# Two transformer layers on one core: three kinds of loads are ordered behind a transpose, and layer 2's first raw weights get a buffer of their own

## The chip, the cores and the metric

The kernel runs on one core of a Trainium2 chip. The metric is the device time of one execution in microseconds (us); lower is better. The engines are TensorE (PE in the profile, its weight loads PEld), VectorE (DVE), ScalarE (ACT), GpSimd (POOL) and SyncE (SP). All DMA transfers of this kernel are issued by SP, from one queue and in order.

## The reference, cut to what matters

```python
D_MODEL = 1024; SEQ = 1024; DEPTH = 2; HEAD_DIM = 64; N_HEADS = 16; BLOCK = 128
DSWA_GROUPS = ((128, 1), (512, 4), (2048, 16))

def reference(x, positions, ...):
    for i in range(DEPTH):
        h = rms_norm(x, norm_g[i])
        if i == 0:
            o, gate = fox_mixer(h, ...)      # layer 1
        else:
            o, gate = dsw_mixer(h, ...)      # layer 2
        x = x + (o * silu(gate)) @ w_out

def fox_mixer(h, w_in, b_f, q_g, k_g):       # q, k, v, gate and forget logits from h @ w_in
    c = cumsum(log_sigmoid(f_logit), axis=1)
    # causal, per head:  p = softmax(q k^T / 8 + c_q - c_k);  o = p v

def dsw_mixer(h, cos, sin, w_in, q_g, k_g):  # q, k, v for each of three dilated windows
    # per window g: rotary q and k, banded softmax with its log-sum-exp, o_g = p v
    # o = sum over g of softmax_g(lse_g) * o_g
```

Everything is float32. The kernel reaches that precision with a high and a low part of each operand.

## The kernel before, in words

The sequence is eight tiles of 128 rows. The projections use the input transposed (`xh`, `xl`: high and low part). A "unit" is one slab of 384 weight columns (q, k and v of a pair of heads) projected for the eight tiles: `project` does 24 matmuls per tile, and a unit has 192 of them.

Layer 1 (the "fox" layer, up to about 660 us with its output projection) has eight such units, one per head pair `hp`. Besides the projection, TensorE works on the attention of head pairs whose projections are done: scores `s` (L450), whose bias row `bc` (L624, the cumulated forget logits of one head, broadcast to 128 partitions) VectorE adds while it takes the maximum (L658); ScalarE's exponential; the split of the exponentials into f16 high and low (`ph`, ScalarE L495 and GpSimd L498); a DMA transpose of `ph` into `ptt` (L499, in `p_transpose`); and the product with the values (`o`, L506 to L508). Query tile t needs t + 1 blocks of keys, so tile 7 has the largest transposes: one of 128x16x128 for each head of the pair, first e = 0, then e = 1. Queries and keys reach TensorE by another DMA transpose, `hl` into `qk_t` (L430, made for two tiles at a time).

Layer 2 (the dilated windows) has 24 units: eight of window 0, and then for each head pair one of window 2 and one of window 1. A transpose `ptt` is made there too (L913). The sum over windows uses `og_d` and `cmb`. The unit that ends window 0 reads the input again in another order (`reload_x`: tiles `x2`). The last unit, for the output projection, loads rows of the mixed result (`turn_y`: tiles `yt`, 128x512, L711) and TensorE transposes them (L346).

Each unit's weights come in four loads of 384 KB, `load(0)` to `load(3)`, into tiles `raw` (two buffers), in the unit before the one that uses them. VectorE takes a maximum of each (`bound`, `vm`, L258), and each half of a `raw` is split into a high and a low part (`w`: ScalarE L289, then GpSimd or VectorE L291).

What sets the order: on TensorE the order is that of the program, written by hand with a clock of ticks (`Flow`): a tile's projection is four ticks, and `flow.at(slot, fn)` puts a piece of work at a tick. The order on the other engines, SP's queue among them, is set by a scheduler with its own estimates. Each tag of a pool has a fixed number of buffers: the tag `ga` holds `bc` (layer 1, 7 buffers), and in layer 2 `x2` and `yt` (4 buffers). A DMA waits for the work that fills its source and for the last readers of the buffer that it overwrites; what stands behind it in SP's queue waits with it.

Of the kernel before, what the change touches and what calls it, by code (L numbers as in the profile page):

```python
# [2 lines left out]

# [1 line left out]

# [17 lines left out]
P = 128  # L23
# [3 lines left out]
NT = S // P  # L27
NH = 16
HD = 64
NHP = NH // 2  # L30
# [52 lines left out]
def trunk(ctx, tc, ins, out, cfg):  # L83
    nc = tc.nc
# [20 lines left out]
    flow = Flow()  # L105

    layer = {}

    def next_layer(bufs):
        if layer:  # L110
# [5 lines left out]
    def lay(shape, dtype, name, tag):  # L116
        return layer["pool"].tile(shape, dtype, name=name, tag=tag, bufs=layer["bufs"][tag])
# [9 lines left out]
    c_d = dram.tile([NH, S], F32, name="c_d")  # L127
# [110 lines left out]
    class Weights:  # L238
# [7 lines left out]
                self.vm2 = sm.tile([P, KT // 2], F32R, name="vm2", tag="vm2")  # L246

        def load(self, i, tag=None):
            if tag is None:
                self.raw[i] = w_p.tile([P, 2, 384], F32, name="raw", tag="raw", bufs=2)  # L250
            else:
                self.raw[i] = lay([P, 2, 384], F32, name="raw", tag=tag)
            nc.sync.dma_start(self.raw[i][:, :, : self.n], self.src[:, 2 * i : 2 * i + 2, :])

        def bound(self, i):
            if self.vcols is None:
# [230 lines left out]
    def p_transpose(ne, nk, exps, splits):  # L487

        ph = lay([P, ne, 2, nk], F16, name="ph", tag="ph")
        pt = lay([P, ne * 2 * nk // P, P], F16, name="ptt", tag="ptt")  # L490
        for p, acc in exps:
            nc.scalar.activation(p, p, AF.Exp, bias=acc, scale=-1.0)  # L492
        for e, cols, p, pool_l in splits:
            if cfg["ph"]:
                nc.scalar.copy(ph[:, e, 0, cols], p)  # L495
            else:
                nc.vector.tensor_copy(ph[:, e, 0, cols], p)
            (nc.gpsimd if pool_l else nc.vector).tensor_sub(ph[:, e, 1, cols], p, ph[:, e, 0, cols])  # L498
        nc.sync.dma_start_transpose(pt, ph.rearrange("p e a k -> p (e a k)"))  # L499
        return pt.rearrange("p (e a k) s -> p e a k s", a=2, e=ne)  # L500

    def pv(o, e, blocks, vt):
# [116 lines left out]
    bcs = {}  # L619

    def load_bc(hp, h, es=(0, 1)):
        for e in es:
            bcs[hp, e, h] = lay([P, 512], F32, name="bc", tag="ga")
            nc.sync.dma_start(bcs[hp, e, h], c_d[2 * hp + e, h * 512 : (h + 1) * 512].partition_broadcast(P))  # L624

    def fox_tile(hp, t, kts, vt, sl):
        LP = cfg["lpf"]
        nk = (t + 1) * P
        st = {}
        pieces = [(a, min(a + 512, nk)) for a in range(0, nk, 512)]  # L630
        both = len(pieces) == 1
        accs = {}
        ptl = {}
        ps = {0: [], 1: []}

        def score(e, c):
            a, b = pieces[c]
            if e == 0 and c == 0:
                gs = st["gs"] = lay([P, P], F32, name="gsf", tag="gsl")
                nc.sync.dma_start(gs, gs_d[t * P : (t + 1) * P, hp * P : (hp + 1) * P])  # L640
            if c == 0:
                accs[e] = BIG
                st["acc"] = sm.tile([P, 2], F32, name="acc", tag="acc", bufs=8)
            if t < 2:
                if e == 0:
                    st["p"] = lay([P, 2, nk], F32, name="p", tag="p")
                p = st["p"][:, e]
            else:
                p = lay([P, b - a], F32, name="p", tag="p")
            ps[e].append(p)  # L650
            s = ps_s.tile([P, 512], F32, name="s", tag="s")
            runs = [(kts[j // 2], j % 2, n) for j, n in key_runs(range(a // P, b // P))]
            scores(s, kts[t // 2], t % 2, e, runs, b < nk)
            if b == nk:

                nc.tensor.matmul(s[:, t * P - a : b - a], ident_b, tri_b, start=False, stop=True, skip_group_check=True)
            acc = st["acc"][:, c : c + 1]
            nc.vector.tensor_tensor_reduce(p, s[:, : b - a], bcs[hp, e, a // 512][:, : b - a], -1.0, accs[e], ALU.add, ALU.min, acc)  # L658
            accs[e] = acc
            pl = (cfg["pl"] & 1, cfg["pl"] >> 1 & 1)  # L660
            if c < len(pieces) - 1 or both and e == 0:
                return
            if both:
                exps = [(ps[i][0], accs[i]) for i in range(2)]
                if t < 2:
                    splits = [(slice(0, 2), slice(0, nk), st["p"], pl[1])]
                else:
                    splits = [(i, slice(0, nk), ps[i][0], pl[i]) for i in range(2)]
                pt = p_transpose(2, nk, exps, splits)
                for i in range(2):  # L670
                    ptl[i] = [(pt[:, i, 0, j], pt[:, i, 1, j], j) for j in range(t + 1)]
            else:
                exps = [(p, accs[e]) for p in ps[e]]
                splits = [(0, slice(*pieces[i]), ps[e][i], pl[i]) for i in range(2)]
                pt = p_transpose(1, nk, exps, splits)
                ptl[e] = [(pt[:, 0, 0, j], pt[:, 0, 1, j], j) for j in range(t + 1)]

        def values(e):
            if e == 0:
                st["o"] = ps_o.tile([P, 2, HD + 1], F32, name="o", tag="o")  # L680
            pv(st["o"], e, ptl[e], vt)
            if e == 1:
                finish()

        def finish():
            o = st["o"]
            rec = sm.tile([P, 2], F32, name="rec", tag="rec")
            nc.vector.reciprocal(rec, o[:, :, HD])
            y = sb.tile([P, P], F32, name="y", tag="y")
            for e in range(2):  # L690
                nc.vector.scalar_tensor_tensor(y[:, e * HD : (e + 1) * HD], o[:, e, :HD], rec[:, e : e + 1], st["gs"][:, e * HD : (e + 1) * HD], ALU.mult, ALU.mult)
            if hp == NHP - 1:
                turn_last(y, t, flow.now + 3)
            else:
                nc.sync.dma_start(y_d[t * P : (t + 1) * P, hp * P : (hp + 1) * P], y)


        ts, tv = cfg["fox"][both]
        for e in range(2):
            for c in range(len(pieces)):  # L700
                urgent(lambda e=e, c=c: score(e, c), "ps", sl + ts[e * len(pieces) + c])
            urgent(lambda e=e: values(e), "pv", sl + LP + tv[e])
# [29 lines left out]
    for hp in range(NHP):  # L732
        w2 = (fox_weights(hp + 1) if hp + 1 < NHP else part(w_fo, 0)).ahead()
        s0 = flow.now
        if hp == 0:
            load_bc(0, 0)
        for h, e, slot in cfg["bc"]:
            if hp + 1 - h < NHP:
                flow.at(s0 + slot, lambda n=hp + 1 - h, h=h, e=e: load_bc(n, h, (e,)))
        kts = []  # L740
        vt = v_tile(w.vs)
        vsr = sm.tile([P, NT], F32, name="vsr", tag="vsr")
        nc.scalar.activation(vsr, rx[:, 0], AF.Copy, scale=w.vs)
        for t in range(NT):
            ps = project(w, tile_cols(0, t))
            if t % 2 == 0:
                hd = heads_begin()
            heads_tile(ps, 0, t, hd, vt, vsr[:, t : t + 1], rx[:, 2, t - 1 : t + 1])
            if t % 2:
                with tc.high_priority(cfg["ph_"]):  # L750

                    turn = heads_pair(0, t - 1, hd)
                    flow.at(flow.now + (6 if hp < NHP - 1 else 4), lambda turn=turn, kts=kts: kts.append(turn()))
                for i in range(2):

                    tt = t - 1 + i
                    fox_tile(hp, tt, kts, vt, s0 + (cfg["due"][tt] if hp < NHP - 1 else 4 * tt + 18))
            if hp == NHP - 1:

                a = max(flow.now + 1, s0 + cfg["due"][t] - 4 * NT + cfg["lpf"] + 9)  # L760
                turn_y(t, 0, [(flow.now + 1, flow.now + 8), (a, a + 7)])
        w = w2
# [229 lines left out]
    for ci, (hp, g) in enumerate(order):  # L992
        w2 = (dsw_weights(ci + 1) if ci + 1 < len(order) else part(w_do, 0)).ahead()
        vt = v_tile(w.vs)
# [3 lines left out]
        for t in range(NT):  # L998
            if ci == NHP - 1:
                reload_x(t)  # L1000
            ps = project(w, tile_cols(g, t))
# [20 lines left out]
            else:  # L1022
                cmb = {}
# [31 lines left out]
    layer["cm"].__exit__(None, None, None)  # L1055


CFG = dict(pin=1, bc=((1, 0, 26), (1, 1, 28), (0, 0, 38), (0, 1, 46)), wl=(0x50, 0x50), ps=0, pv=100, ph_=100, ph=1, wbufs=12, pl=3, um=3, lpf=8, lsd=((16, 16), (16, 14), (14, 11)), ty2=((0, 4), (1, 5)), hb=1, ub=2, qb=1, nb=3, fox=(((0, 0, 2, 2), (2, 4)), ((0, 0), (4, 4))), due=(29, 33, 39, 45, 35, 41, 49, 57), l1=dict(ga=7, ptt=3, ph=2, p=4, qk_t=6, vt=3, gsl=3), l2=dict(ga=4, cmb=3, ptt=3, ph=2, p=2, qk_t=3, og=3, vt=3, gsl=3, par=1), wload=(0, 4, 13, 20), wbound=(9, 14, 22, 27), wscale=28, wsplit=(10, 11, 15, 16, 29, 29, 30, 30))


def host_layout(inputs):
# [49 lines left out]
```

## Time and profile before

| | |
|---|---|
| median of 3 runs | 1816.11 us (1810.0 to 1819.2) |
| profiled execution | 1818.5 us, span 1816.7 us |
| TensorE | busy 1737.0 us, 96% of the span |
| VectorE, ScalarE, GpSimd | 60%, 56%, 54% |
| DMA, from SP's queue | 652996 packets, 288.36 MB, 71.4% of the 16 engines' span |
| layer 1's attention units | 193 to 468 us |
| layer 2's units of windows 2 and 1 | 1082 to 1717 us, the output projection from there to the end |

How to read the rows that follow: a row of the timeline has the start in us, the duration, the engine and line, the operation with its output and input tiles, and in brackets the idle time of that engine just before and what ended it. On SP ("SPq") the duration is that of issuing a DMA, not of its transfer. A granted clock of 1.00 is TensorE's full clock.

### The profile page before, as it was taken

How to read it: one execution, taken by the hardware profiler on the slowest of the kernel's cores; microseconds unless marked ns; L12 is line 12 of the kernel's file. 1: busy time of each engine (PE TensorE's matmuls, PEld its weight loads, DVE VectorE, ACT ScalarE, POOL GpSimd, SP SyncE). 2: the span in 40 equal slices, each digit the busy share in tenths (PEclk: the TensorE clock that was granted, in tenths of full speed). 3: DMA queues.
4: the chain of work that ended last, by engine and by line, in shares of the span. 5: the costliest groups of instructions: out<-in, count | busy, mean ns of one | idle time of the engine just before them, and what ended most of it. 6: DMA issues, size and time to landing. Idle time of an engine off the chain costs nothing.

```text
span 1816.7 us, 38150 instructions
## 1 busy us (share of the span) xinstructions
PE 1737.0 (96%) x13276; PEld 1641.7 (90%) x13276; DVE 1093.3 (60%) x3674; ACT 1011.0 (56%) x2696; POOL 973.5 (54%) x1175
## 2 busy tenths in 40 slices
PE   7999999999988989999999999999999999999999
PEld 6999888888876779999999989999999999999877
DVE  8546666666664453365556585666675666667631
ACT  6536666666665465455555665555555555555620
POOL 4215565556545431255656566667576666757530
PEclk9999999999999999999999999999999999999999
DMA  8447999999999763456767687667677776667852
GB/s 285 127 130 140 193 190 185 176 177 183 187 190 207 213 188 114 127 113 134 142 133 144 146 191 143 157 140 152 138 163 144 162 151 143 149 140 179 189 154 85
DMA packets 653189, 290.79 MB, mean 160 GB/s; under 512 B 512306, under 2 KB 616754, under 8 KB 652996
## 3 DMA queue, kind: packets, MB, share of 16 engines
q1 hardware_dynamic: 652996, 288.36, 71.4%
q8 instruction: 104, 1.70, 0.4%
q14 instruction: 89, 0.73, 0.1%
HBM read 126.46 MB, written 37.03 MB: 90 GB/s over the span
## 4 chain that ended last, share of the span: by engine, by line
PE 45%; DMA 12%; DVE 6%; ACT 4%; issue 3%; POOL 3%; SPq 1%; DVEq 0%; POOLq 0%; ACTq 0%
PE pj L313 33%; PE pj L336 7%; DMA raw<-in_w_dsw 5%; PE s L450 2%; DMA qk_t<-hl 2%; DMA ptt<-ph 2%; DMA og_d<-og 1%; POOL hl L425 1%; POOL w L291 1%; DMA cmb<-og_d 1%; DVE w L291 1%; DVE hl L426 1%; DVE u L422 1%; PE ob L506 1%; DVE p L906 1%
## 5 line engine op out<-in xcount | busy, mean ns | idle before, releaser
L313 PE MATMUL pj<-w,xh 128*128 128x384 f32 (+2 forms) x4864 | 1259.6, 341 | 30.2 <-ACT w L289 7.3
L313 PEld LDWEIGHTS pj<-w,xh 128*128 128x128 f32 x4864 | 873.1, 191 | 38.9 <-DVE ge L481 7.8
L313 PE MATMUL pj<-w,xl 128*128 128x384 f32 (+2 forms) x2432 | 817.6, 336 | 0.2 <-DVE xl L530 0.2
L313 PEld LDWEIGHTS pj<-w,xl 128*128 128x128 f32 x2432 | 464.7, 191 | 0.9 <-DVE xl L530 0.9
L291 POOL TENSOR_TENSOR w<-raw,w 128x384 fp32r<-128x384 f32 (+2 forms) x258 | 261.7, 1035 | 233.3 <-ACT w L289 228.8
L498 POOL TENSOR_TENSOR ph<-p,ph 128x512 f16<-128x512 f32 (+3 forms) x176 | 172.9, 999 | 161.9 <-ACT ph L495 160.7
L289 ACT CAST w<-raw 128x384 fp32r<-128x384 f32 (+2 forms) x352 | 162.6, 501 | 114.8 <-PE pj L336 37.4
L425 POOL TENSOR_TENSOR hl<-u,hl 128x512 f16<-128x512 f32 x128 | 151.2, 1181 | 125.0 <-ACT hl L424 124.9
L912 POOL TENSOR_TENSOR ph<-p,ph 128x768 f16<-128x768 f32 (+2 forms) x96 | 155.3, 1618 | 102.9 <-ACT ph L911 102.9
L383 ACT ACTIVATE sq<-pj 128x256 f32<-128x256 f32 x256 | 97.2, 380 | 168.9 <-DVE u L378 167.2
L450 PE MATMUL s<-qk_t 128*128 128x128 f16 (+1 forms) x1504 | 162.0, 248 | 19.2 <-DVE acc L658 10.4
L336 PE MATMUL pj<-xh,w 128*128 128x512 f32 x512 | 170.4, 404 | 2.2 <-ACT p L907 1.1
L258 DVE TENSOR_REDUCE vm<-raw 128x1 f32<-128x256 f32 x128 | 53.6, 419 | 156.2 <-DMA raw<-in_w_dsw 118.6
L506 PEld LDWEIGHTS <-ptt 128*128 128x128 f16 x1136 | 102.9, 98 | 48.8 <-issue 27.5
L389 DVE SCALAR_TENSOR_TENSOR vt<-pj,vsr,vt 128x128 f16<-128x128 f32 x256 | 89.6, 350 | 93.2 <-ACT vt L388 92.8
L450 PEld LDWEIGHTS <-qk_t 128*128 128x128 f16 x1504 | 110.2, 98 | 36.1 <-issue 22.0
L424 ACT CAST hl<-u 128x512 f16<-128x512 f32 x128 | 79.2, 619 | 104.9 <-DVE u L422 88.6
L495 ACT CAST ph<-p 128x512 f16<-128x512 f32 (+3 forms) x176 | 88.9, 537 | 72.7 <-DMA ptt<-ph 72.3
L492 ACT ACTIVATE p<-p,acc 128x512 f32<-128x512 f32 (+2 forms) x192 | 109.0, 609 | 30.6 <-DVE acc L658 27.4
L336 PEld LDWEIGHTS pj<-xh,w 128*128 128x128 f32 x512 | 97.6, 191 | 24.5 <-DVE xr L779 1.5
L378 DVE TENSOR_TENSOR u<-pj,gr 128x256 f32<-128x256 f32 x256 | 106.4, 416 | 18.4 <-PE pj L313 18.3
L907 ACT ACTIVATE p<-p,og 128x128 f32<-128x128 f32 (+1 forms) x256 | 98.1, 441 | 33.6 <-DVE og L906 33.4
(171 smaller groups left out, 2609.4 us busy)
## 6 DMA issues: line engine op xcount, KB each, us to landing
raw<-in_w_dsw SPq DMA_DIRECT2D x96, 384.0 KB, 3.7
raw<-in_w_fox SPq DMA_DIRECT2D x32, 384.0 KB, 3.7
og_d<-og SPq DMA_DIRECT2D x64, 132.0 KB, 3.2
cmb<-og_d SPq DMA_DIRECT2D x64, 132.0 KB, 3.3
bc<-c_d SPq DMA_DIRECT2D x32, 256.0 KB, 3.9
gs_d<-ge SPq DMA_DIRECT2D x32, 192.0 KB, 3.2
xt<-in_xt SPq DMA_DIRECT2D x16, 256.0 KB, 6.1
xrow<-in_x SPq DMA_DIRECT2D x8, 512.0 KB, 6.3
```

Of the source, the lines that this page charges most:

```text
L289: nc.scalar.copy(w[:, 0, :n], raw[:, k % 2, :n])
L291: eng.tensor_sub(w[:, 1, :n], raw[:, k % 2, :n], w[:, 0, :n].bitcast(F32))
L313: nc.tensor.matmul(ps[:, :n], a[:, k, cols], w.slabs[k][:, j, :n], start=(k == 0 and i == 0), stop=(k == KT - 1 and i == 2))
L336: nc.tensor.matmul(ps[m], w.slabs[k][:, j, m * P : (m + 1) * P], a[:, k, 512 * b : 512 * (b + 1)], start=(k == 0 and x == 0), stop=(k == K ...
L378: nc.vector.tensor_mul(u[:, t % 2].rearrange("p (a b) d -> p a b d", a=2), ps[:, : 4 * HD].rearrange("p (a b d) -> p a b d", a=2, b=2), gr ...
L425: nc.gpsimd.tensor_sub(hl[:, :, :4, 1], u, hl[:, :, :4, 0])
L450: nc.tensor.matmul(s[:, c0 : c0 + cnt * P].rearrange("p (c s) -> p c s", c=cnt), qk[:, i, blk], kk[:, j : j + cnt, e], start=(h == 0), sto ...
L492: nc.scalar.activation(p, p, AF.Exp, bias=acc, scale=-1.0)
L498: (nc.gpsimd if pool_l else nc.vector).tensor_sub(ph[:, e, 1, cols], p, ph[:, e, 0, cols])
L506: nc.tensor.matmul(o[:, e, :], hi, vt[:, j, e, HD:], start=(b == 0), stop=False, skip_group_check=True)
L907: nc.scalar.activation(p[:, e], p[:, e], AF.Exp, bias=acc[:, e : e + 1], scale=-1.0)
L912: nc.gpsimd.tensor_sub(ph[:, 1], st["p"], ph[:, 0])
```

## The change

`tc.issue_after(x)` orders what is issued inside it behind the instruction x on the same queue; it adds no wait. The change keeps the transpose `ptt` of tile 7, e = 1 of the latest head pair in `last["late"]`, and puts behind it, on SP: the first weight load of each unit, the `bc` loads of the first half of the sequence (h = 0), and the `qk_t` transpose of tiles 6 and 7. `last["late"]` keeps its value in layer 2, where it has long been issued. In layer 2 `load(0)` goes to a tag of its own, `raw0`, with one buffer, so a unit has three `raw` buffers in place of two, and `ga` shrinks from four buffers to two.

```diff
+    def queued():
+        return tc.issue_after(last["late"]) if "late" in last else nullcontext()
...
         def load(self, i, tag=None):
+            if i == 0 and tag is None and "raw0" in layer["bufs"]:
+                tag = "raw0"
             if tag is None:
                 self.raw[i] = w_p.tile([P, 2, 384], F32, name="raw", tag="raw", bufs=2)
             else:
                 self.raw[i] = lay([P, 2, 384], F32, name="raw", tag=tag)
-            nc.sync.dma_start(self.raw[i][:, :, : self.n], self.src[:, 2 * i : 2 * i + 2, :])
+            with queued() if i == 0 else nullcontext():
+                nc.sync.dma_start(self.raw[i][:, :, : self.n], self.src[:, 2 * i : 2 * i + 2, :])
...
-        nc.sync.dma_start_transpose(pt, ph.rearrange("p e a k -> p (e a k)"))
+        last["ptt"] = nc.sync.dma_start_transpose(pt, ph.rearrange("p e a k -> p (e a k)")).ins
...
             bcs[hp, e, h] = lay([P, 512], F32, name="bc", tag="ga")
-            nc.sync.dma_start(bcs[hp, e, h], c_d[...].partition_broadcast(P))
+            with queued() if h == 0 else nullcontext():
+                nc.sync.dma_start(bcs[hp, e, h], c_d[...].partition_broadcast(P))
...
                 pt = p_transpose(1, nk, exps, splits)
+                if t == NT - 1 and e == 1:
+                    last["late"] = last["ptt"]
...
-                    flow.at(flow.now + (6 if hp < NHP - 1 else 4), lambda turn=turn, kts=kts: kts.append(turn()))
+                def turned_keys(turn=turn, kts=kts, t=t):
+                    with queued() if t == NT - 1 else nullcontext():
+                        kts.append(turn())
+                flow.at(flow.now + (6 if hp < NHP - 1 else 4), turned_keys)
...
-... l2=dict(ga=4, cmb=3, ptt=3, ... par=1), ...
+... l2=dict(ga=2, cmb=3, ptt=3, ... par=1, raw0=1), ...
```

TensorE's order of instructions is the same before and after. The scheduler sets the others anew. Line numbers of the changed kernel are up to 17 higher (L430 is L439, L499 is L508, L624 is L634, L253 is L262).

Place one: SP's queue at the end of a layer 1 unit (near 245 us in the trace). `ptt_3286` and `ptt_3347` are tile 7's two transposes, e = 0 and e = 1; `raw_3500` is a unit's first weight load. Before:

```order
L640 DMA gsf_3421<-gs_d_88 128x128
L624 DMA bc_3666<-c_d_87 128x512
L624 DMA bc_3907<-c_d_87 128x512
L624 DMA bc_4239<-c_d_87 128x512
L430 DMA_TRANSPOSE qk_t_3455<-hl_3224 128x12x128
L695 DMA y_d_83<-y_3411 128x128
L499 DMA_TRANSPOSE ptt_3286<-ph_3285 128x16x128
L253 DMA raw_3500<-in_w_fox 128x768
L499 DMA_TRANSPOSE ptt_3347<-ph_3346 128x16x128
L499 DMA_TRANSPOSE ptt_3437<-ph_3436 128x4x128
```

and after:

```order
L650 DMA gsf_3421<-gs_d_88 128x128
L439 DMA_TRANSPOSE qk_t_3455<-hl_3224 128x12x128
L707 DMA y_d_83<-y_3411 128x128
L508 DMA_TRANSPOSE ptt_3286<-ph_3285 128x16x128
L650 DMA gsf_3502<-gs_d_88 128x128
L508 DMA_TRANSPOSE ptt_3347<-ph_3346 128x16x128
L508 DMA_TRANSPOSE ptt_3437<-ph_3436 128x4x128
L262 DMA raw_3500<-in_w_fox 128x768
L262 DMA raw_3592<-in_w_fox 128x768
L634 DMA bc_3666<-c_d_87 128x512
L634 DMA bc_3907<-c_d_87 128x512
```

Three `bc` loads and the first weight load have moved behind tile 7's transposes; `qk_t_3455` and the `y` store stay ahead of them.

Place two: GpSimd in a unit of window 1 of layer 2 (near 1396 to 1405 us). `ra`, `rb` and the line that writes `u` are the rotary step; `w_20120` to `w_20173` are low parts of the next unit's weights, of which `raw_19960` is the first load. Before:

```order
L940 TENSOR_TENSOR cmb_19747<-cmb_19747 128x4x65
L410 TENSOR_TENSOR ra_19928<-u_19838,cs_114 128x128
L411 TENSOR_TENSOR rb_19929<-u_19838,sn_115 128x8x8
L412 TENSOR_TENSOR rb_19929<-u_19838,sn_115 128x8x8
L936 TENSOR_TENSOR wt_20131<-mm_20129,cmb_19897 128x12
L413 TENSOR_TENSOR u_19838<-ra_19928,rb_19929 128x8x16
L912 TENSOR_TENSOR ph_19916<-p_19896,ph_19916 128x768
```

and after:

```order
L957 TENSOR_TENSOR cmb_19747<-cmb_19747 128x4x65
L300 TENSOR_TENSOR w_20120<-raw_19960,w_20120 128x384
L419 TENSOR_TENSOR ra_19928<-u_19838,cs_114 128x128
L420 TENSOR_TENSOR rb_19929<-u_19838,sn_115 128x8x8
L421 TENSOR_TENSOR rb_19929<-u_19838,sn_115 128x8x8
L300 TENSOR_TENSOR w_20136<-raw_19960,w_20136 128x384
L953 TENSOR_TENSOR wt_20131<-mm_20129,cmb_19897 128x12
L929 TENSOR_TENSOR ph_19916<-p_19896,ph_19916 128x768
L300 TENSOR_TENSOR w_20173<-raw_19991,w_20173 128x384
L422 TENSOR_TENSOR u_19838<-ra_19928,rb_19929 128x8x16
```

Three weight splits and the split of the exponentials now stand ahead of the last step of the rotary.

Place three: SP's queue in the last unit (near 1685 us). `yt_24248` and `yt_24259` are rows of tile 1, `yt_24405` and `yt_24407` those of tile 2. Before, tile 1's two loads stand far ahead, and here is:

```order
L430 DMA_TRANSPOSE qk_t_24088<-hl_24083 128x12x128
L913 DMA_TRANSPOSE ptt_24198<-ph_24197 128x8x128
L711 DMA yt_24405<-y_d_83 128x512
L711 DMA yt_24407<-y_d_83 128x384
L430 DMA_TRANSPOSE qk_t_24226<-hl_24221 128x12x128
L1018 DMA og_d_89<-og_24040 128x264
```

and after:

```order
L439 DMA_TRANSPOSE qk_t_24088<-hl_24083 128x12x128
L930 DMA_TRANSPOSE ptt_24198<-ph_24197 128x8x128
L723 DMA yt_24248<-y_d_83 128x512
L723 DMA yt_24259<-y_d_83 128x384
L439 DMA_TRANSPOSE qk_t_24226<-hl_24221 128x12x128
L1035 DMA og_d_89<-og_24040 128x264
L723 DMA yt_24405<-y_d_83 128x512
L723 DMA yt_24407<-y_d_83 128x384
```

Tile 1's loads stand where tile 2's stood, since only two `yt` are held at a time.

More of the change, by code (lines that the diff above doesn't have):

```diff
@@ L1 @@
 import heapq
-from contextlib import ExitStack
+from contextlib import ExitStack, nullcontext
 import numpy as np
@@ L107, in trunk @@
     layer = {}
+    last = {}
+    def queued():
+        return tc.issue_after(last["late"]) if "late" in last else nullcontext()
     def next_layer(bufs):
@@ L623, in load_bc @@
             bcs[hp, e, h] = lay([P, 512], F32, name="bc", tag="ga")
-            nc.sync.dma_start(bcs[hp, e, h], c_d[2 * hp + e, h * 512 : (h + 1) * 512].partition_broadcast(P))
+            with queued() if h == 0 else nullcontext():
+                nc.sync.dma_start(bcs[hp, e, h], c_d[2 * hp + e, h * 512 : (h + 1) * 512].partition_broadcast(P))
     def fox_tile(hp, t, kts, vt, sl):
@@ L1055, in trunk @@
     layer["cm"].__exit__(None, None, None)
-CFG = dict(pin=1, bc=((1, 0, 26), (1, 1, 28), (0, 0, 38), (0, 1, 46)), wl=(0x50, 0x50), ps=0, pv=100, ph_=100, ph=1, wbufs=12, pl=3, um=3, lpf=8, lsd=((16, 16), (16, 14), (14, 11)), ty2=((0, 4), (1, 5)), hb=1, ub=2, qb=1, nb=3, fox=(((0, 0, 2, 2), (2, 4)), ((0, 0), (4, 4))), due=(29, 33, 39, 45, 35, 41, 49, 57), l1=dict(ga=7, ptt=3, ph=2, p=4, qk_t=6, vt=3, gsl=3), l2=dict(ga=4, cmb=3, ptt=3, ph=2, p=2, qk_t=3, og=3, vt=3, gsl=3, par=1), wload=(0, 4, 13, 20), wbound=(9, 14, 22, 27), wscale=28, wsplit=(10, 11, 15, 16, 29, 29, 30, 30))
+CFG = dict(pin=1, bc=((1, 0, 26), (1, 1, 28), (0, 0, 38), (0, 1, 46)), wl=(0x50, 0x50), ps=0, pv=100, ph_=100, ph=1, wbufs=12, pl=3, um=3, lpf=8, lsd=((16, 16), (16, 14), (14, 11)), ty2=((0, 4), (1, 5)), hb=1, ub=2, qb=1, nb=3, fox=(((0, 0, 2, 2), (2, 4)), ((0, 0), (4, 4))), due=(29, 33, 39, 45, 35, 41, 49, 57), l1=dict(ga=7, ptt=3, ph=2, p=4, qk_t=6, vt=3, gsl=3), l2=dict(ga=2, cmb=3, ptt=3, ph=2, p=2, qk_t=3, og=3, vt=3, gsl=3, par=1, raw0=1), wload=(0, 4, 13, 20), wbound=(9, 14, 22, 27), wscale=28, wsplit=(10, 11, 15, 16, 29, 29, 30, 30))
 def host_layout(inputs):
```

## The prediction

> **What bounds the kernel now.** I read the page's busy times first, then the chain, then what TensorE waits for.
>
> ```profile
> span 1816.7 us, 38150 instructions
> PE 1737.0 (96%) x13276; PEld 1641.7 (90%) x13276; DVE 1093.3 (60%) x3674; ACT 1011.0 (56%) x2696; POOL 973.5 (54%) x1175
> ...
> PE pj L313 33%; PE pj L336 7%; DMA raw<-in_w_dsw 5%; PE s L450 2%; DMA qk_t<-hl 2%; DMA ptt<-ph 2%; DMA og_d<-og 1%; POOL hl L425 1%; POOL w L291 1%; DMA cmb<-og_d 1%; DVE w L291 1%; DVE hl L426 1%; DVE u L422 1%; PE ob L506 1%; DVE p L906 1%
> ```
>
> TensorE bounds it. Nothing in the change takes a matmul away, so all that can be gained is its idle time, 1816.7 - 1737.0 = 79.7 us, and the matmuls that run slow because the clock has dropped. The chain names loads and transposes that the change moves, but only with 2 to 5% each. The waits of TensorE by cause (us in all, times, longest):
>
> ```profile
> PE o L506 <- DMA ptt<-ph: 16.8, 11, 3.6
> PE s L450 <- DVE acc L658: 10.4, 10, 2.0
> ...
> PE pj L313 <- DVE u L422: 6.0, 7, 1.6
> ```
>
> The largest is the one that the first part of the change is near: the product with the values waiting for a transpose. Where in layer 1 the idle time lies is told by a table by unit (start and end, length, then busy time of PE, and at the end of the row the granted clock, the busy share of the DMA engines and GB/s):
>
> ```profile
> 143.76:192.93 49.17, 48.73 (x458) 45.64 (x458) 33.28 (x122) 33.00 (x83) 28.68 (x30) 1.00 0.90 179
> 192.93:247.35 54.42, 50.62 (x506) 47.09 (x506) 35.42 (x127) 35.22 (x91) 32.48 (x33) 1.00 0.98 186
> 247.35:301.40 54.05, 50.76 (x507) 47.22 (x507) 34.63 (x124) 34.46 (x87) 31.69 (x33) 1.00 0.94 184
> 301.40:357.25 55.85, 51.99 (x506) 48.61 (x506) 35.89 (x130) 35.38 (x91) 32.78 (x33) 0.97 0.90 181
> ...
> 411.45:467.76 56.31, 52.04 (x506) 48.55 (x506) 36.68 (x130) 36.35 (x93) 33.51 (x34) 0.97 0.98 181
> ```
>
> Each of the last four has 3.3 to 4.3 us of idle time. Two of them have a lower clock as well, and their PE time is 1.3 us longer for the same 506 matmuls. The timeline shows why (TensorE rows, idle time before them in brackets):
>
> ```profile
> 252.63 0.20 PE L506 MATMUL o<-vt,ptt 128*128 128x65 f16 x1 [1.36 <-DMA ptt<-ph]
> ...
> 308.26 0.20 PE L506 MATMUL o<-vt,ptt 128*128 128x65 f16 x1 [2.92 <-DMA ptt<-ph]
> ...
> 311.99 0.80 PE L313 MATMUL pj<-w,xh 128*128 128x384 f32 x2
> 312.63 0.34 PE L313 MATMUL pj<-w,xl 128*128 128x384 f32 x1
> 312.80 0.52 PE L313 MATMUL pj<-w,xh 128*128 128x384 f32 x2
> ...
> 417.82 0.20 PE L506 MATMUL o<-vt,ptt 128*128 128x65 f16 x1 [2.46 <-DMA ptt<-ph]
> ```
>
> After the wait of 1.36 us nothing happens to the clock. After 2.92 us a pair of matmuls takes 0.80 us until 312.8, and 0.52 from there: the last slow ones of a stretch of about 3.4 us, in which matmuls run at half the rate, about 1.5 us lost. The wait of 2.46 us is followed by the same stretch. So I price a wait of over some 2 us at 1.5 us more.
>
> The Trainium skill ("TensorE: Matmul & The Clock Gate", the table of what matters for kernels) asks for no idle gaps over about 3 us, and Part 1 gives an idle window of about 3.4 us ahead of half rate. Here 2.46 us was enough, so the trace differs. By the page neither of these waits would cost more than itself, and the sum below would be a gain of 2.6 - 1.5 = 1.1 us without the clock in layer 1, and 1.1 + 1.5 = 2.6 us if the page is kept in the tail as well.
>
> **The change part by part.** *Layer 1, the queue.* SP's rows ahead of the wait at 252.63, and VectorE's wait behind the same load:
>
> ```profile
> 241.97 1.33 SPq L624 DMA_DIRECT2D bc<-c_d  x3
> 245.56 1.43 SPq L430 DMA_TRANSPOSE qk_t<-hl  x1
> 247.08 1.11 SPq L695 DMA_DIRECT2D y_d<-y  x1
> 248.28 1.84 SPq L499 DMA_TRANSPOSE ptt<-ph  x1
> 250.22 1.02 SPq L253 DMA_DIRECT2D raw<-in_w_fox  x1
> 251.34 4.40 SPq L499 DMA_TRANSPOSE ptt<-ph  x2
> ...
> 254.54 0.42 DVE L258 TENSOR_REDUCE vm<-raw 128x1 f32<-128x256 f32 x1 [3.19 <-DMA raw<-in_w_fox]
> ```
>
> Two things move: three `bc` loads of 256 KB from ahead of the first transpose of tile 7, and the weight load from between the two. The second is plain: the weight load's 1.02 us of issue go from ahead of the second transpose, and that transpose's own issue (two rows in 4.40 us, of which 1.20 is the small one) should fall from 3.1 to about 1.8 us, as the first has. That brings e = 1 some 2 us earlier. But TensorE hardly waits for it: 252.63 is e = 0. For e = 0 the three stay that stand right ahead (`qk_t`, `y`, itself), 1.43 + 1.11 + 1.84 = 4.38 us; only the transfers of `bc`, still under way when `qk_t` is issued, go. In the unit from 301.40 the last two took 0.53 and 1.32 us, so up to 1.1 us of this is backlog of the DMA engines; transposes keep these 0.9 to 0.98 busy in any case, so I take half, 0.6 us, at six unit ends: 3.6 us. I add one clock stretch (the wait of 2.46 us comes under 2 us): 1.5 us. VectorE's 3.19 us wait for the weights goes from this place, and `acc` with it; of the 10.4 us that TensorE waits for `acc` I take 0.5. Layer 1: -5.6 us. Bounds: no gain at all, if the engines' backlog stays; and five waits (10 us, two of 2.92 and 2.46 among them) gone with both stretches and 2 us of `acc`, -15.
>
> The moved loads have cover. A unit's first weights are split some 10 ticks later and used a unit later (50 us); `bc` for the first half is used from the next unit's middle; `qk_t` of tiles 6 and 7 is used by tile 6 and 7's scores, the next unit's work. Should the cover of the second weight pair fail (its buffer waits for the splits of the first, now later), the transposes behind it on SP are held up by about 1 us: within the bounds.
>
> *Layer 2, first weights a unit ahead.* Rows of a unit of window 1:
>
> ```profile
> 1395.86 2.35 POOL L291 TENSOR_TENSOR w<-raw,w 128x384 fp32r<-128x384 f32 x2
> 1398.55 0.89 SPq L253 DMA_DIRECT2D raw<-in_w_dsw  x2
> 1400.03 0.48 POOL L413 TENSOR_TENSOR u<-ra,rb 128x128 f32<-128x128 f32 x1
> 1401.06 1.66 POOL L912 TENSOR_TENSOR ph<-p,ph 128x768 f16<-128x768 f32 x1 [0.56 <-ACT ph L911]
> 1403.97 0.42 DVE L258 TENSOR_REDUCE vm<-raw 128x1 f32<-128x256 f32 x1 [0.58 <-DMA raw<-in_w_dsw]
> 1405.11 0.69 DVE L422 TENSOR_TENSOR u<-u,pj 128x512 f32<-128x512 f32 x1
> 1405.94 0.60 PE L313 MATMUL pj<-w,xh 128*128 128x384 f32 x2 [1.58 <-DVE u L422]
> ...
> 1160.00:1670.00 510.00, 501.36 (x3728) 489.39 (x3726) 345.65 (x1284) 283.05 (x863) 346.15 (x476) 1.00 0.69 151
> ```
>
> Two loads are issued together, VectorE waits for both, and the rotary product behind it is late for TensorE. With the first load a unit ahead, the second still comes in at the same place, so `vm` of it still waits to about 1403. And the early weights let the scheduler put their splits ahead of the rotary on GpSimd. From its free time at 1398.9 (0.75 us of `cmb` after the row at 1395.86): one split 0.97, rotary 1.13, split and `wt` 1.20, `ph` 1.66, split 0.97, then the last step 0.48: it ends at 1405.3 in place of 1400.5, about where VectorE starts the product now. So the wait changes its cause more than its size. In thirteen units from 1160 to 1670 all idle time is 510.00 - 501.36 = 8.6 us. I take -1.5; bounds -7 and +4.
>
> *Layer 2, two buffers for `x2`.* In the unit from 1036 to 1082 us each `x2` load must wait for the splits of two loads before. That chain (a load of about 3.5 us, a copy and a subtraction of 0.6 and 0.7) is about as long as a tile's 5.2 us of projection. SP's other work queues behind those waits. +1, bounds 0 and +3.
>
> *Layer 2, two buffers for `yt`.* The loads of tile 1 move from 1649 to 1653 to the place after the transpose at 1684.84:
>
> ```profile
> 1653.32 1.00 SPq L711 DMA_DIRECT2D yt<-y_d  x1
> ...
> 1684.84 1.23 SPq L913 DMA_TRANSPOSE ptt<-ph  x1
> 1686.17 1.01 SPq L711 DMA_DIRECT2D yt<-y_d  x2
> ...
> 1685.92 0.63 PE L346 MATMUL pt<-ident,yt 128*128 128x128 f32 x4
> ...
> 1712.59 1.09 PE L346 MATMUL pt<-ident,yt 128*128 128x128 f32 x4 [2.61 <-issue]
> ...
> DMA to landing us min/median/max: 2.3/3.5/4.8
> ```
>
> TensorE turns tile 1 at 1685.92. With the load issued at 1686.2 and 3.4 us to land, it waits to about 1689.5: 3.6 us, long enough for a clock stretch, 1.5 more. Part comes back, since work that waits later (2.61 us at 1712.59) gets time: I take 1.6. Net +3.5; bounds +1 and +6.
>
> Sum: -5.6 - 1.5 + 1 + 3.5 = -2.6 us. The profiled execution took 1818.5 us (1.8 around its span), so 1815.9 for such a one; it stands 2.4 above the median of 1816.1, so 1813.5.
>
> **The rivals.** (1) *Nothing in layer 1.* For it: the DMA engines are 0.90 to 0.98 busy there, and order does not make less work; also `qk_t` and `y` stay ahead of e = 0. Against it: the waits are latency of one transfer, and VectorE's wait of 3.19 us does go. Then 3.0 in layer 2 alone: -1.5 + 1 + 3.5, 1819 us.
>
> (2) *All of the waits for tile 7 go.* For it: the issue of 1.84 and 3.1 us against 1.2 for the small transpose shows a backlog, and both long waits bring clock stretches with them. -15 in layer 1, -3 in layer 2's units, +1, +3.5: -13.5, so 1818.5 - 13.5 - 2.4 = 1802.6.
>
> (3) *Slower: the rotary behind the splits.* Place: GpSimd's last rotary step in the units of window 1. It decides once this step ends 0.5 us later than 1405.3, for then TensorE's 1.58 us become over 2 and the clock drops: 0.5 + 1.5 = 2 us in each of eight units, 16 us. 1813.5 + 16 = 1829.5. For it: the sum of durations above leaves no slack. Against it: the scheduler may have kept the slack in other units, and the wait for `vm` ends nearly 1 us earlier (its load is now issued first, at 1398.55).
>
> **How the numbers follow.** About 0.5%, 9 us, is what a measurement of this kernel can tell from no change (the three runs lie 9 us apart). My forecast has 0.45, rival 1 0.20, rival 2 0.22, rival 3 0.13. Faster than 1807: rival 2 and 0.05 from the forecast's lower edge, 0.27. Slower than 1825: rival 3, 0.13. The rest, 0.60, is within. The range takes in rival 1 and most of rival 2's side, and leaves rival 3 and the extreme of 2 out: 1804 to 1822.
>
> **What would show it.** Right: in the units from 193 to 468 us TensorE waits for `ptt` under 2 us each and the two clocks of 0.97 become nearer to 1; the second transpose of tile 7 is issued in under 2 us; VectorE no longer waits 3 us for `in_w_fox` there; near 1686 us a new wait of about 3.6 us of TensorE's transposes for `yt`; in window 1's units the wait for the rotary stays between 1 and 2 us. It is wrong if the waits for `ptt` keep their size (rival 1), vanish (2), or if the sum of waits for the rotary grows past 12 us (3).

## The result, and the profile after

The changed kernel is slower: 1826.82 us in the median of 15 runs (1820.19 to 1832.84) against 1815.52 of 15 runs before; the ratio is 1.0061, with an interval from 1.0050 to 1.0072. I had forecast 1813.5, within 1804 to 1822. The profiled execution has a span of 1828.2 us, 11.5 more than before. The page's busy times, and the waits of TensorE (us in all, times, longest):

```profile
span 1828.2 us, 38050 instructions
PE 1741.3 (95%) x13276; PEld 1647.4 (90%) x13276; DVE 1091.4 (60%) x3674; ACT 1011.6 (55%) x2696; POOL 977.6 (53%) x1175
```

```profile
PE o L515 <- DMA ptt<-ph: 17.1, 8, 3.8
PE s L459 <- DMA qk_t<-hl: 13.8, 9, 2.6
PE s L459 <- DVE acc L668: 10.0, 9, 1.7
PE pt L355 <- DMA yt<-y_d: 6.7, 3, 2.8
...
PE pj L322 <- DVE u L431: 1.3, 3, 0.7
```

Two of these rows before the change:

```profile
PE s L450 <- DMA qk_t<-hl: 3.5, 5, 1.2
...
PE pt L346 <- DMA yt<-y_d: 2.1, 1, 2.1
```

The wait for the transposed exponentials, at which the first part of the change is aimed, has not shrunk (16.8 before). The wait for the rotary product has (6.0 to 1.3). In its place stand waits for `qk_t`, 13.8 us against 3.5 (7.0 of them in the units from 1126 to 1675 us, 5.6 in the two units before), and for `yt`, 6.7 against 2.1 (the new one of 2.8 in the last unit; the other two are in layer 1's output projection). TensorE itself is busy 4.3 us longer with the same matmuls: more of them run at the lower clock (mean granted clock 0.985 against 0.990).

Four stretches of the same work, first before, then after (start and end, length, PE busy, and at the end clock, DMA share, GB/s). They are five units of layer 1, the `x2` unit with its successor, the units up to the last, and the last:

```profile
192.93:467.76 274.83, 256.07 (x2526) 238.59 (x2526) 177.21 (x631) 175.99 (x444) 162.39 (x162) 0.99 0.95 183
```

```profile
1036.27:1122.42 86.15, 82.20 (x653) 80.00 (x651) 61.20 (x189) 55.49 (x148) 52.48 (x61) 0.98 0.77 167
1122.42:1668.93 546.51, 537.84 (x3994) 525.04 (x3992) 365.03 (x1368) 303.30 (x925) 365.05 (x505) 1.00 0.69 151
1668.93:1717.00 48.07, 44.53 (x319) 42.58 (x317) 30.95 (x103) 28.80 (x82) 24.84 (x35) 0.96 0.84 182
```

```profile
192.81:467.24 274.43, 257.02 (x2526) 240.26 (x2526) 179.43 (x631) 175.25 (x442) 161.76 (x161) 0.98 0.93 184
```

```profile
1034.19:1126.08 91.89, 83.98 (x653) 81.09 (x651) 62.18 (x189) 56.25 (x150) 51.25 (x61) 0.96 0.80 164
1126.08:1675.22 549.14, 538.85 (x3994) 526.52 (x3992) 358.88 (x1365) 302.81 (x924) 366.24 (x504) 1.00 0.68 149
1675.22:1728.33 53.11, 46.91 (x319) 44.80 (x317) 30.33 (x101) 30.00 (x86) 26.46 (x37) 0.91 0.75 167
```

Layer 1 gains 0.4 us; the other three lose 5.7, 2.6 and 5.0. The rest of the program differs by 1 to 2 us a stretch in both directions (the last head pair with layer 1's output projection +2.1, the start -0.1, the gate -1.7, window 0 -2.0, the end +0.1), and stretches differ by that much and more from one profile to another where no edit acts: the last head pair with its output projection took 191.8 us before and 185.7 in ga2_only, which leaves layer 1 as it was. So the losses of 5.7 and 5.0 us stand out by their size and because losses of 5.3 to 7.4 and 2.2 to 5.0 us come back in every run of the table with two buffers and the splits' order of before; the 2.6 by itself does not.

A correction to the texts ahead: the unit at 1396 to 1405 us is one of window 2 (it starts at 1393.47), not of window 1. A unit of window 2 begins while the last pair of a window-1 unit is still at its rotary.

### The profile page after: what moved, and what is told of

Its sections match the earlier page's. It is cut to its first block, busy times and chain, and to the rows that moved or that the text cites. A ratio compares the mean times of both kernels' runs of the same rounds, so it can differ in the third digit from the quotient of the medians.

```text
span 1828.2 us, 38050 instructions
## 1 busy us (share of the span) xinstructions
PE 1741.3 (95%) x13276; PEld 1647.4 (90%) x13276; DVE 1091.4 (60%) x3674; ACT 1011.6 (55%) x2696; POOL 977.6 (53%) x1175
## 4 chain that ended last, share of the span: by engine, by line
PE 57%; DMA 17%; POOL 8%; DVE 7%; ACT 6%; issue 4%; SPq 1%; POOLq 0%; ACTq 0%; DVEq 0%
PE pj L322 42%; PE pj L345 8%; DMA ptt<-ph 5%; PE s L459 3%; POOL w L300 3%; DMA qk_t<-hl 3%; DMA raw<-in_w_dsw 3%; POOL ph L507 2%; POOL hl L434 2%; ACT p L501 1%; ACT ph L504 1%; DMA raw<-in_w_fox 1%; DVE p L668 1%; DMA og_d<-og 1%; ACT w L298 1%
## 5 line engine op out<-in xcount | busy, mean ns | idle before, releaser
L300 POOL TENSOR_TENSOR w<-raw,w 128x384 fp32r<-128x384 f32 (+2 forms) x258 | 267.3, 1053 | 209.7 <-ACT w L298 206.5
L459 PE MATMUL s<-qk_t 128*128 128x128 f16 (+1 forms) x1504 | 161.9, 248 | 26.8 <-DMA qk_t<-hl 13.8
L433 ACT CAST hl<-u 128x512 f16<-128x512 f32 x128 | 79.2, 618 | 116.7 <-DVE u L431 93.6
L435 DVE COPY hl<-hl 128x512 f16<-128x512 f16 x128 | 68.6, 536 | 91.9 <-POOL hl L434 91.8
```

The lines of the kernel that those rows point to most:

```text
L300: eng.tensor_sub(w[:, 1, :n], raw[:, k % 2, :n], w[:, 0, :n].bitcast(F32))
L459: nc.tensor.matmul(s[:, c0 : c0 + cnt * P].rearrange("p (c s) -> p c s", c=cnt), qk[:, i, blk], kk[:, j : j + cnt, e], start=(h == 0), sto ...
```

## The experiments

In the table each ratio is against the kernel before on the same chip (with its interval). It is not the quotient of the two medians; for ga2_only that would be 1.0072. Medians are compared only within a chip, ratios across chips. The three stretches are of the profiled execution, in us: the `x2` unit and its successor, the units up to the last, the last. The profiled execution of ga2_only was its fastest of six, 1820.65 us, so its stretches are rather short.

| kernel | edges on SP | ga | raw0 | splits behind rotary | median us | ratio | x2 | units | last |
|---|---|---|---|---|---|---|---|---|---|
| before | no | 4 | no | no | | 1 | 86.2 | 546.5 | 48.1 |
| ga2_only | no | 2 | no | no | 1831.06 | 1.0057 (1.0036, 1.0078) | 93.6 | 544.0 | 50.3 |
| q_only | yes | 4 | no | no | 1820.78 | 1.0021 (1.0009, 1.0034) | 86.3 | 545.7 | 47.4 |
| raw0_only | no | 2 | yes | no | 1827.08 | 1.0044 (1.0032, 1.0056) | 91.5 | 547.7 | 52.0 |
| after | yes | 2 | yes | no | 1826.82 | 1.0061 (1.0050, 1.0072) | 91.9 | 549.1 | 53.1 |
| rope_only | no | 4 | no | yes | 1803.03 | 0.9933 (0.9908, 0.9957) | 82.7 | 543.8 | 45.8 |
| q_rope | yes | 4 | no | yes | 1807.19 | 0.9949 (0.9934, 0.9964) | 82.9 | 541.8 | 46.9 |
| rope_ga2 | no | 2 | no | yes | 1810.25 | 0.9964 (0.9949, 0.9979) | 86.8 | 541.1 | 49.4 |
| raw0_rope | no | 2 | yes | yes | 1810.68 | 0.9955 (0.9943, 0.9967) | 86.4 | 541.7 | 46.9 |
| after_rope | yes | 2 | yes | yes | 1815.39 | 1.0003 (0.9988, 1.0018) | 85.6 | 546.0 | 46.9 |

**The parts alone.** Theory 1 after the result: the loss is layer 2's. The edits are the change's own lines, taken out one by one:

```diff
-        return tc.issue_after(last["late"]) if "late" in last else nullcontext()   # raw0_only, ga2_only
+        return nullcontext()
-l2=dict(ga=2, ... raw0=1)      # q_only: ga=4, no raw0;  ga2_only: ga=2, no raw0
```

> Only the ordering edges behind tile 7's transpose; four ga buffers and no raw0 in layer 2, as before. Theory 1 (the loss is layer 2's: fewer buffers for x2 and yt, and splits that go ahead of the rotary) expects 1814 to 1817 us, the attention units from 193 to 467 us within 1 us of before in sum. Rival (the edges themselves cost, in the last head pair, whose stretch to the end of layer 1 became 2.1 us longer) expects 1820 us or more.

> Only the cut of ga from four buffers to two in layer 2; no edges, no raw0. Theory 1a (the buffers are the larger cost) expects 1821 to 1825 us: the last unit near 53 us in place of 48, and 2 to 4 us in the two units from 1036 us. Rival 1b (the early weights' splits on GpSimd are the larger cost) expects 1819 us at most.

> Layer 2's part alone: raw0 with one buffer and ga with two; no edges. Theory 1 expects all of the loss to be here: 1824 to 1829 us, with the waits for qk_t in the units from 1160 to 1670 us (7 us in the changed kernel). The rival that the edges cost expects 1820 us or less.

The edges cost 0.2% and gain nothing. The median, 1820.78 us, reaches the rival's 1820, on a chip where the kernel before took 1817.96; by the ratio it lies between the two expectations. The five units of layer 1 take 275.3 us, and the last head pair with its output projection 192.1 against 191.8, so the rival's place is not confirmed. Two buffers alone cost 0.57%, nearly the whole loss, in the places named for theory 1a but not in its sizes: 7.4 us in the `x2` units (2 to 4 expected), 50.3 in the last unit (53 expected), and a median of 1831 above its 1821 to 1825. Layer 2's part alone costs 0.44%, within theory 1's range. So the loss is mainly that of the two buffers. `raw0` adds waits for `qk_t` after 1160 us (6.6 us in raw0_only, 0.4 in ga2_only), and 3.7 us in the units there, but no time on the whole that can be told: 1.0044 against 1.0057, with overlapping intervals.

**GpSimd's order.** The chain in the changed kernel, in the window-2 unit from 1240.13 us (GpSimd, then SP and TensorE):

```profile
1244.35 1.03 POOL L300 TENSOR_TENSOR w<-raw,w 128x384 fp32r<-128x384 f32 x1
1245.34 0.46 POOL L419 TENSOR_TENSOR ra<-u,cs 128x128 f32<-128x128 f32 x1
...
1246.32 1.03 POOL L300 TENSOR_TENSOR w<-raw,w 128x384 fp32r<-128x384 f32 x1
...
1247.48 1.66 POOL L929 TENSOR_TENSOR ph<-p,ph 128x768 f16<-128x768 f32 x1
1249.11 1.00 POOL L300 TENSOR_TENSOR w<-raw,w 128x384 fp32r<-128x384 f32 x1
1250.07 0.45 POOL L422 TENSOR_TENSOR u<-ra,rb 128x128 f32<-128x128 f32 x1
...
1255.39 1.17 POOL L434 TENSOR_TENSOR hl<-u,hl 128x512 f16<-128x512 f32 x1
```

```profile
1258.08 1.44 SPq L439 DMA_TRANSPOSE qk_t<-hl  x1
```

```profile
1261.80 0.83 PE L459 MATMUL s<-qk_t 128*128 128x128 f16 x8 [1.61 <-DMA qk_t<-hl]
```

Three splits stand ahead of the rotary's last step, as the order had shown. That step starts 9.9 us into the unit; the split of `hl`, the transpose, and the scores follow late, and TensorE waits for the scores' operand. The product at which I had looked no longer waits. Over the eight window-2 units the last rotary step starts 9.3 us into the unit on average, 5.4 before the change, since mostly five splits stand ahead of it in place of two. But ahead of `hl` it is mostly six both times, and the transpose is issued 16.2 us into the unit, 15.8 before; what waits are the units in which it is later than the average, as in this one. The test takes the early splits behind the rotary and leaves everything else:

```diff
-            nc.gpsimd.tensor_add(u[:, :, :, :ROT], ra, rb)
+            last["rope"] = nc.gpsimd.tensor_add(u[:, :, :, :ROT], ra, rb).ins
...
-            eng.tensor_sub(w[:, 1, :n], raw[:, k % 2, :n], w[:, 0, :n].bitcast(F32))
+            with tc.issue_after(last["rope"]) if k < 2 and eng is nc.gpsimd and "rope" in last else nullcontext():
+                eng.tensor_sub(w[:, 1, :n], raw[:, k % 2, :n], w[:, 0, :n].bitcast(F32))
```

> As raw0_only, and GpSimd's splits of each unit's first weight load are ordered behind the latest rotary step (no wait is added). Theory 1b (these splits ahead of the rotary make qk_t late) expects 5 to 8 us less than raw0_only and no waits for qk_t over 0.5 us from 1160 to 1670 us. Theory 1a expects the same time as raw0_only within 2 us.

The same work in raw0_rope, whose unit starts at 1235.29 us, and the waits for `qk_t` in raw0_only and raw0_rope:

```profile
1240.11 0.45 POOL L420 TENSOR_TENSOR ra<-u,cs 128x128 f32<-128x128 f32 x1
...
1241.64 1.67 POOL L930 TENSOR_TENSOR ph<-p,ph 128x768 f16<-128x768 f32 x1 [0.33 <-ACT ph L929]
1243.26 0.46 POOL L423 TENSOR_TENSOR u<-ra,rb 128x128 f32<-128x128 f32 x1
...
1247.31 1.17 POOL L435 TENSOR_TENSOR hl<-u,hl 128x512 f16<-128x512 f32 x1
```

```profile
1249.92 1.44 SPq L440 DMA_TRANSPOSE qk_t<-hl  x1
```

```profile
PE s L459 <- DMA qk_t<-hl: 13.8, 10, 2.6
```

```profile
PE s L460 <- DMA qk_t<-hl: 2.5, 2, 1.6
```

The transpose is issued 14.6 us into the unit in place of 18.0 (13.9 in place of 16.2 on average), with four splits ahead of `hl` in place of six. The waits fall from 13.8 us to 2.5, and none is left from 1160 to 1670 us. The time falls by 16.4 us between the medians, twice what I expected: the units gained 6.0 us, and the `x2` and last units as well, from 91.5 to 86.4 and from 52.0 to 46.9 us, where one stretch of 3.4 us at the lower clock is left of four. That the order of these splits makes `qk_t` late is shown. That it is the cause of the change's loss is not: the kernel before may pay for the same order, which rope_only asks.

> The changed kernel whole, and GpSimd's splits of the first load behind the latest rotary step. If the splits ahead of the rotary are the changed kernel's main loss, 1808 to 1814 us, no wait for qk_t over 0.6 us from 1160 to 1670 us. If the two ga buffers are, 1821 or more.

With this order the whole change stands at 1.0003 against a kernel before that does not have it. No wait for `qk_t` is left from 1160 to 1670 us. The time is 1.4 us above the first range.

> The kernel before with only the order of GpSimd's splits behind the rotary (four ga buffers, no raw0, no edges on SP). If the early weights are what gained in raw0_rope, this is within 4 us of before (1814 to 1820). If the order of the splits alone gained, it is near 1811.

The order without the change is the best kernel of all, 0.67% faster than before, 8 us beyond its second expectation. In the kernel before, too, splits stood ahead of `hl`: two ahead of the rotary's last step and these four behind it:

```profile
1247.79 3.89 POOL L291 TENSOR_TENSOR w<-raw,w 128x384 fp32r<-128x384 f32 x4
1251.63 0.77 POOL L940 TENSOR_TENSOR cmb<-cmb 128x260 f32<-128x260 f32 x1
1252.33 1.20 POOL L425 TENSOR_TENSOR hl<-u,hl 128x512 f16<-128x512 f32 x1
```

In raw0_rope two of them do (1.96 us). Of the 14.0 us between the two profiles 3.4, 2.8 and 2.2 are in the three stretches and 2.3 in window 0 (274.5 us, as in every run with this order but raw0_rope_ga3, against 276.8); the rest is in stretches where no edge acts.

This changes what the order explains. The change costs 0.61% without it (1.0061 against 1) and 0.70% with it (1.0003 against 0.9933). The order gains about as much in the kernel before (0.67%) as in the changed one (0.58%), so both paid for it: it makes up for the change's loss, and as far as these runs can tell it is not the cause of that loss.

> As rope_only, with two ga buffers in layer 2 in place of four (no raw0). If the two buffers are what raw0_rope loses against rope_only (7.7 us between their medians), 1808 to 1813 us, the loss in the units from 1036 to 1120 and in the last one. If raw0 itself is, 1805 us at most.

> As rope_only, with the change's edges on SP (four ga buffers, no raw0). If the edges cost by themselves, as after_rope against raw0_rope says, 1806 to 1809 us. If they are free, 1801 to 1805 us.

On this base the two buffers cost 0.31% (4.1 us in the `x2` units, 3.5 in the last), the edges 0.16%, and `raw0` given two buffers nothing that can be told: 0.9955 against 0.9964. The intervals of both rope_ga2 and q_rope overlap that of rope_only, so these sizes are loose; ga2_only and q_only have the same signs. The rest of the 0.70% comes in when the edges are put on top of raw0_rope: after_rope is 0.48% slower, and there the intervals do not overlap. Why the edges cost more there than alone is open, and `raw0` with four buffers was not run.

> As rope_only, with the splits of the second load too behind the latest rotary step. If splits ahead of the rotary are still a cost there, 1797 to 1801 us; if the first load's were all that mattered, as rope_only within 3 us; if GpSimd then lacks time for the splits later in the unit, waits of the projection for w appear and it is slower than 1806.

```diff
-            with tc.issue_after(last["rope"]) if k < 2 and eng is nc.gpsimd and "rope" in last else nullcontext():
+            with tc.issue_after(last["rope"]) if k < 4 and eng is nc.gpsimd and "rope" in last else nullcontext():
```

Holding back the second load's splits too costs: 1828.17 us, ratio 1.0059 (1.0038 to 1.0079), with 564.4 us in the units up to the last. TensorE then waits for the rotary product (9.9 us in all, 4.9 in rope_only), for `vt` (7.8 against 0.8), and for GpSimd's `w` (5.3 against 0.9), the last as I had written for the case that GpSimd lacks time. `qk_t` is no earlier for it: its transpose is issued 14.1 us into the window-2 units, 14.0 in rope_only. How much each of these costs is not settled; the scheduler's whole order is another one.

> As raw0_rope, with a third ga buffer (paid for by one og buffer less). If what is left of the two buffers' cost is the waits for x2 and yt (about 7 us of TensorE's waits in raw0_rope from 1050 to 1085 and from 1680 to 1725 us), 1805 to 1809 us; if those waits are covered by others, as raw0_rope (1809 to 1812).

This gave 1859.11 us, 1.0251 (1.0223 to 1.0279), and does not answer its question. All units of layer 2 became longer, those of window 0 with no `x2` or `yt` too (296.4 us against 274.5): `og` with two buffers in place of three is the only other difference from raw0_rope, so the buffer that paid for the third `ga` was worth more.

**Layer 1: what the first transpose waits for.** SP after the change, at the same unit end as in the prediction:

```profile
245.27 1.45 SPq L439 DMA_TRANSPOSE qk_t<-hl  x1
246.81 0.89 SPq L707 DMA_DIRECT2D y_d<-y  x1
247.78 1.91 SPq L508 DMA_TRANSPOSE ptt<-ph  x1
249.75 0.99 SPq L650 DMA_DIRECT2D gsf<-gs_d  x1
250.82 3.83 SPq L508 DMA_TRANSPOSE ptt<-ph  x2
```

With no `bc` in flight the first transpose's issue takes 1.91 us (1.84 before), so `bc` was not its backlog. What stayed ahead was `qk_t` and the `y` store. The test, on the kernel before, moves these two behind it:

```diff
+                if t == NT - 1 and e == 0:
+                    last["early"] = last["ptt"]
...
+                    with tc.issue_after(last["early"]) if t == NT - 3 and "early" in last else ...:
                         kts.append(turn())
...
+                with tc.issue_after(last["early"]) if "early" in last else nullcontext():
                     nc.sync.dma_start(y_d[...], y)
```

> The kernel before with another order in layer 1 only: the y stores and the qk_t transpose of tiles 4 and 5 go behind tile 7's first transpose (e = 0) on SP; bc and the weights are not ordered. If e = 0 is late because those two stand ahead of it (they take about 3 us of SP), the five waits for it (10 us in 193 to 468 us) fall under 1 us each and the sum of the five units by 8 us or more, 1806 to 1811 us. If the DMA engines' load sets it, they stay, and the time is that of before within 3 us.

```profile
PE s L459 <- DMA qk_t<-hl: 12.4, 12, 1.9
...
PE o L515 <- DMA ptt<-ph: 4.2, 3, 2.9
```

The waits for `ptt` fall from 16.8 to 4.2 us, so the place in the queue did set them; but TensorE's next need is the `qk_t` that now stands behind, and waits for it rise from 3.5 to 12.4. The five units take 272.9 us, 1.9 less where 8 or more were expected, and the whole 1817.99, ratio 1.0018 (1.0000 to 1.0035). Both transposes are wanted within a few us of each other, and one queue issues them.

## Why the prediction was wrong, point by point

**Layer 1, -5.6 forecast, -0.4 measured.** The step that failed is the half of 1.1 us taken as backlog of `bc` for e = 0. Its issue did not get shorter. I had noted that `qk_t` and `y` stay ahead; that was the whole answer, as early shows. The second transpose was to be issued in 1.8 us and took 2.6 (3.83 less 1.2), behind a small load in place of the weights. The five waits for e = 0 went from 10.0 to 8.9 us. The clock stretch that I had counted as saved was not: three of these units have a clock of 0.97 in place of two. VectorE's wait for the weights moved from 3.19 to 1.53 us, but TensorE's waits for `acc`, of which I had taken 0.5 us off, rose by 0.6. Rival 1, to which I gave 0.20, was right for layer 1.

**Window 2 and 1, -1.5 forecast, +2.6 measured, within -7 to +4.** The wait for the product went, as the change would have it; rival 3 had the place and the cause on GpSimd (splits ahead of the rotary), but named the wrong waiter: the last rotary step came 3.9 us later on average, the product no longer waited, and the waits came out at `qk_t`, whose transpose is at most 17.9 us into its unit. I followed the chain to one consumer and stopped. The ordering in raw0_rope takes these waits away, so their cause is shown; but the 2.6 us are little against what stretches differ by, and rival 3's 16 us came only in part. That the whole time, 1826.8 us, lies near rival 3's 1829.5 is luck, since most of the loss is that of the buffers.

**Two buffers for `x2`, +1 forecast, +5.7 measured, outside 0 to +3.** The term was mis-sized, since I priced the chain of `x2` by itself. What stands behind its wait on ScalarE is the row that was missing:

```profile
1082.37 0.62 ACT L1004 CAST xh<-x 128x512 fp32r<-128x512 f32 x1 [2.15 <-DMA x<-xn_d]
1082.89 1.34 ACT L298 CAST w<-raw 128x384 fp32r<-128x384 f32 x3
1084.14 0.61 ACT L433 CAST hl<-u 128x512 f16<-128x512 f32 x1
```

```profile
1094.02 1.89 PE L459 MATMUL s<-qk_t 128*128 128x128 f16 x12 [2.56 <-DMA qk_t<-hl]
```

ScalarE waits 2.15 us for an `x2` load, then makes the splits' high parts, and only then `hl`; GpSimd puts three splits (3.53 us, from 1083.48) ahead of `hl` there, and `qk_t` is 2.56 us late, in a clock stretch of 3.4 us. In ga2_only, with the same two buffers and no `raw0`, the two units are longer still, and it is another consumer that is late. VectorE's `xl`, also made from an `x2` load, takes 2.20 us ahead of `vt`, and TensorE waits for `vt`:

```profile
1091.33 2.20 DVE L1005 TENSOR_TENSOR xl<-x,xh 128x512 fp32r<-128x512 f32 x1 [0.55 <-ACT xh L1004]
1093.45 0.34 DVE L398 SCALAR_TENSOR_TENSOR vt<-pj,vsr,vt 128x128 f16<-128x128 f32 x1
```

```profile
1093.84 1.01 PE L322 MATMUL pj<-w,xh 128*128 128x384 f32 x2 [3.57 <-DVE vt L398]
```

So the loss goes with the buffers, and which wait shows it goes with the order. With the order of the splits changed, the two units take 86.4 us with two buffers in raw0_rope and 82.7 with four in rope_only.

**Two buffers for `yt`, +3.5 forecast, +5.0 measured, within +1 to +6.** Place and mechanism were right (SP, then TensorE):

```profile
1691.81 1.01 SPq L723 DMA_DIRECT2D yt<-y_d  x2
```

```profile
1695.15 1.09 PE L355 MATMUL pt<-ident,yt 128*128 128x128 f32 x4 [2.78 <-DMA yt<-y_d]
```

The wait is 2.78 us, not 3.6, with the lower clock behind it (0.91 in the last unit, 0.96 before). What I had counted as given back was not: a later wait of 2.6 us is still there. In raw0_rope one of the two loads stands one transpose earlier in SP's queue, and the wait is 1.15 us, as it should be if the place in the queue sets it. In the sum a wait taken 0.8 us too long stands against 1.6 us that were not given back, so the net 3.5 came out nearer than its parts by luck.

**The sum.** -2.6 was forecast, +11.5 is what the profiles show: the terms were too low by 5.2 in layer 1, 4.1 in window 2 and 1, 4.7 in `x2` and 1.5 in `yt`, and the stretches that no term was for give 1.4 back. All four erred to the same side. Two workings in the prediction do not follow from its own figures: the 0.60 was worked out for 1807 to 1825 us, not for the range that is given; and the gain of 2.6 us by the page's rule leaves out a clock stretch in the tail, though the wait forecast there, 3.6 us, is longer than both figures that are quoted.

## What to carry to other kernels

When an added order makes a changed kernel faster, add it to the kernel before as well: a cost that both carry does not explain their difference. Taking the buffers that pay for a new one away by themselves is the other run to make first; here that alone lost nearly as much as the whole change. Giving a load its own early buffer does not only end a wait: in a kernel whose order is set by a scheduler, the work that the load feeds becomes ready earlier and can be put ahead of more urgent work on another engine, so look in the order for what has moved ahead of the chain that TensorE waits for, and follow that chain to its last consumer, not to the next one. An order edge for the less urgent work was worth more here (0.6 to 0.7%) than anything in the change, but holding back twice as much of it was worse than holding back none. In one in-order queue, moving something behind a late transfer helps only if it stood ahead of that transfer while the queue was busy; two transfers that are wanted at about the same time mostly exchange their waits.

## What the runs showed of the hardware that I had not expected

A wait of 1.92 us at 307.38 us in the changed kernel was followed by a stretch at the lower clock in a unit with a clock of 0.97, as the waits of 2.46 and 2.92 were before; the Trainium skill's 3 us ("TensorE: Matmul & The Clock Gate", the table of what matters for kernels) is further off than my bound of some 2 us. But the length of one wait does not decide it. In raw0_only the same five waits of layer 1 are longer, 11.1 us together with four of them over 2 us, and all five units have a clock of 1.00. The first of them:

```profile
199.48 0.20 PE L515 MATMUL o<-vt,ptt 128*128 128x65 f16 x1 [2.64 <-DMA ptt<-ph]
```

```profile
192.93:248.31 55.38, 50.60 (x506) 47.07 (x506) 36.44 (x132) 36.15 (x93) 33.37 (x34) 1.00 0.95 187
```

Layer 1 of raw0_only is that of the kernel before, where two of these waits brought a stretch. So 1.5 us for a wait over a bound is no safe price, and what decides whether a wait of 2 to 3 us brings a stretch is open.

The second 128x16x128 transpose took 3.1 us to issue right behind the weights and still 2.6 behind a small load: most of the excess over the 1.2 us of the 128x4x128 one did not go with the weights, and what holds it is open.
